# A feed-forward convolution placed three ticks later, with thirds of 3, 4 and 4 and one gate chunk ahead of the down-projection

## The chip, the cores and the metric

The kernel runs on one core of one Trainium2 chip. The core has a matmul engine (TensorE, PE in the profile), a vector engine (VectorE, DVE), a scalar engine (ScalarE, ACT), GpSimd (POOL) and SyncE (SP). Each takes its instructions in one fixed order and waits where an operand is not ready. ACT, SP and POOL also issue DMA transfers, which run on 16 DMA engines. The metric is the device time of one execution in microseconds; the median of three runs is compared.

## The reference

Two decoder layers over 256 rows of 2048 numbers. In each layer four attention groups are followed by a gated feed-forward block, and the change is in that block alone:

```python
def causal_depthwise_conv(u, w, bias):
    seq = u.shape[1]
    up = jnp.pad(u, ((0, 0), (CONV_WIDTH - 1, 0), (0, 0)))
    out = bias.astype(u.dtype) + up[:, 0:seq] * w[0]
    for j in range(1, CONV_WIDTH):
        out = out + up[:, j:j + seq] * w[j]
    return out

def ffn_sublayer(x, ffn_norm, w_up, conv_w, conv_b, w_down):
    h = rms_norm(x, ffn_norm)
    u = causal_depthwise_conv(h @ w_up, conv_w, conv_b)
    gate, val = jnp.split(u, 2, axis=-1)
    return x + (jax.nn.silu(gate) * val) @ w_down
```

`w_up` is 2048 x 11264: 5632 gate columns, then 5632 value columns. The convolution runs along the 256 rows, with three taps.

## The kernel before

Everything is float32. A product is made of three matmuls in a reduced format: weights and activations are split into a high and a low part, and high x high, low x high and high x low are added (L269 to L271). The activations' parts are made once. The weights' parts are made on the way: ACT casts a pair of weight tiles to the high part (L242, 1024 numbers a partition), DVE subtracts for the low part (L243). Four pairs of parts can be in flight (`wspl`, 4 buffers), and three raw weight loads of 1 MB, each of two pairs (`wraw`, 3 buffers; SP issues them).

A `Gemm` of the up-projection makes one chunk of 512 columns in 8 steps. A step takes one weight pair, issues 12 matmuls, and then calls `tick`. The 22 chunks of a layer are called g_0 to g_10 (gate) and v_0 to v_10 (value), and are taken alternately. A chunk comes out with rows on partitions, while convolution and down-projection want columns on partitions. So each chunk is turned: ACT evacuates it from PSUM with a row scale (L301, tile `v`), DVE transposes 32 x 32 blocks (L845, `T`), one DMA writes `T` to DRAM (L848, `td`) and four DMAs read it back turned (L853, `u`). `conv_T` then computes bias and last tap on ACT (L876), the other two taps on DVE (L878, L880), in two halves of two column blocks each. A gate chunk gets its SiLU (L885). A value chunk is multiplied with its gate chunk and split for the down-projection (L891 to L893, tiles `a0h_f`, `a0l_f` and so on).

What is not a Gemm step is written as tasks (generators). There are two queues: `movers` holds the turns, `queue` the convolutions and what follows them. A tick advances the first task of each queue to its next `yield`, with a bound that its instructions stand no earlier than the last matmul issued (`issue_after`). So a yield is one Gemm step. A scheduler then sets each engine's order from the program's order and those bounds, with its own cost estimates; ACT and DVE make weight parts ahead of TensorE as far as the four buffers go.

The columns are taken in thirds (`THIRDS`): chunks of a third, then its part of the down-projection (`paired`, L806), which adds to x. The down-projection of a third begins two column blocks (three in the last third) with the parts that are there, and takes the last part of each afterwards.

Of the kernel before, what the change touches and what calls it, by code (L numbers as in the profile page):

```python
# [29 lines left out]
NJ = DFF // 512  # L30
# [37 lines left out]
    _o += _w  # L68
CTW = _o

THIRDS = ((0, 4), (4, 8), (8, 11))


@with_exitstack
def tile_trunk(ctx: ExitStack, tc: tile.TileContext, x, xT, pvec, rows, ctab,
# [33 lines left out]
    queue, movers = deque(), deque()  # L109
# [7 lines left out]
    last_mm = [None]  # L117

    def tick(n=1):
        for _ in range(n):  # L120
            for q in (movers, queue):
                if q:
                    with tc.issue_after(last_mm[0].ins):
                        try:
                            next(q[0].gen)
                        except StopIteration:
                            q.popleft().done = True

    def finish(task):
        while task is not None and not task.done:  # L130
            tick()
# [38 lines left out]
    def act_slots(i, n):  # L170
        return slot(i, "h", [P, 4, SEQ], F32R, n), slot(i, "l", [P, 4, SEQ], F32R, n)
# [107 lines left out]
    def wchunk(w, k0=0):  # L279

        def src(raw, k, cnt, q=nc.sync):
            q.dma_start(raw[:, :cnt, :w.shape[2]], w[:, k0 + k:k0 + k + cnt, :])
        return src
# [14 lines left out]
    def evac(acc, n, N, rs, tag, bufs):  # L298
        d = tmp.tile([P, NT, 512], F32, tag=tag, name=f"{tag}_{n}", bufs=bufs)
        for t in range(NT):  # L300
            nc.scalar.activation(d[:, t, :N], acc[t][:, :N], AF.Identity, scale=rs[:, t:t + 1])  # L301
        return d
# [37 lines left out]
    def new_ssq(n):  # L340
        return sml.tile([P, NT, 4], F32, tag="ssq4", name=f"ssq4_{n}")
# [123 lines left out]
    def new_r(n):  # L465
        return sml.tile([P, NT], F32, tag="xs_r", name=f"r_{n}")

    def qk_tile(n):
        return tmp.tile([P, H, SEQ], F32, tag="qkT", name=f"qkT_{n}", bufs=3)
# [6 lines left out]
    for l in range(L):  # L476
# [99 lines left out]
        def gemm512(n, col, r, tag="qk", bufs=2, before=None):  # L576
            acc = Gemm(f"{n}{l}", 512, hT, wc[col], KT).run()
            finish(before)
            return evac(acc, f"{n}{l}", 512, r, tag, bufs)
# [14 lines left out]
        d = gemm512("aq", "aq", rs)  # L594
# [112 lines left out]
        d = gemm512("ak", "ak", rs)  # L707
# [79 lines left out]
        d = gemm512("cq_", "cq", rs, before=t_bq)  # L787
        qcT = qk_tile(f"qc{l}")
        t_cq2 = Task(c_task(d, qcT, l, f"cq_{l}", "cq"))
        d = gemm512("ck_", "ck", rs, before=t_bk)  # L790
# [49 lines left out]
        def turn(u, d, n):  # L840


            T = tmp.tile([P, KT, 32, NT], F32, tag="y", name=f"T_{n}", bufs=1)
            for t in range(NT):
                nc.vector.transpose(T[:, :, :, t], u[:, t, :].rearrange("p (b c) -> p b c", c=32))  # L845
            yield
            td = dram.tile([P, KT * 64], F32, tag="td", name=f"td_{n}")
            nc.scalar.dma_start(td, T.rearrange("p b c t -> p (b c t)"))  # L848
            yield
            yield  # L850
            src = td.rearrange("(a i) (c b x) -> b i c a x", i=32, b=4, x=64)
            for b in range(4):
                nc.scalar.dma_start(d[b * 32:(b + 1) * 32].rearrange("p c (a x) -> p c a x", x=64), src[b])  # L853
            yield
            yield
            yield

        def up(n, j):

            acc = Gemm(f"up_{n}", 512, hT, wchunk(w_up[l, j]), KT).run()  # L860
            u = evac(acc, n, 512, reo, "v", 1)
            d = tmp.tile([P, 4, SEQ], F32, tag="qk", name=f"u_{n}", bufs=2)
            gen = turn(u, d, n)
            next(gen)
            return d, Task(gen, movers)

        def conv_T(u, r, n, half, j):

            d, turned = u
            while not turned.done:  # L870
                yield
            for c in range(4):
                if c == 2:
                    yield
                ch = half * 44 + j * 4 + c
                nc.scalar.activation(r[:, c, :], d[:, c, :], AF.Identity, scale=pcol(l, "cw", 2 * 88 + ch),  # L876
                                     bias=pcol(l, "cb", ch))
                nc.vector.scalar_tensor_tensor(r[:, c, 1:], d[:, c, :SEQ - 1], pcol(l, "cw", 88 + ch), r[:, c, 1:],  # L878
                                               op0=ALU.mult, op1=ALU.add)
                nc.vector.scalar_tensor_tensor(r[:, c, 2:], d[:, c, :SEQ - 2], pcol(l, "cw", ch), r[:, c, 2:],  # L880
                                               op0=ALU.mult, op1=ALU.add)

        def gate_task(d, g, j):
            yield from conv_T(d, g, f"g{l}_{j}", 0, j)
            nc.scalar.activation(g, g, AF.Silu)  # L885

        def val_task(d, v, g, j, hi, lo):
            yield from conv_T(d, v, f"v{l}_{j}", 1, j)
            yield
            for c in (0, 2):  # L890
                nc.vector.tensor_tensor(v[:, c:c + 2, :], v[:, c:c + 2, :], g[:, c:c + 2, :], op=ALU.mult)  # L891
                nc.scalar.copy(hi[:, c:c + 2, :], v[:, c:c + 2, :])
                nc.vector.tensor_tensor(lo[:, c:c + 2, :], v[:, c:c + 2, :], hi[:, c:c + 2, :].bitcast(F32),  # L893
                                        op=ALU.subtract)

        last_layer = l == L - 1
        ssq_x, rs = new_ssq(f"n{l}"), new_r(f"n{l}")
        t_g = t_v = None
        for ti, (j0, j1) in enumerate(THIRDS):
            act, tasks = [], []  # L900
            for j in range(j0, j1):
                d = up(f"g{l}_{j}", j)
                finish(t_g)
                g = qk_tile(f"g{l}_{j}")
                t_g = Task(gate_task(d, g, j))
                finish(t_v)
                d = up(f"v{l}_{j}", NJ + j)
                v = qk_tile(f"v{l}_{j}")
                act.append(act_slots(j - j0, f"f{l}_{j}"))
                t_v = Task(val_task(d, v, g, j, *act[-1]))  # L910
                tasks.append(t_v)

            def post_down(c, acc):
                add_x(c, acc)
                if ti < 2:
                    return
                if last_layer:
                    for t in range(NT):
                        eng = nc.sync if t == 0 else nc.scalar
                        eng.dma_start(out[t * P:(t + 1) * P, c * 512:(c + 1) * 512],  # L920
                                      xs[:, t, c * 512:(c + 1) * 512])
                else:
                    h_task[c] = Task(x_ready(c, f"n{l}", "attn", l + 1, ssq_x, rs))
            nk = (j1 - j0) * 4
            paired(f"dn{l}_{ti}", slotted(act, tasks), w_down[l], j0 * 4, tuple(range(0, nk, 4)), nk, post_down,
                   3 if ti == 2 else 2)
# [72 lines left out]
```

## Time and profile before

| What | Value |
|---|---|
| median of 3 runs | 2359.29 us (2357.53 to 2368.61) |
| the profiled execution | 2353.14 us, with a span of 2351.4 us |
| mean granted clock of TensorE | 0.987 |
| busy: TensorE, DVE, ACT | 2262.7, 1450.2, 1171.0 us |
| HBM traffic over the span | 195 GB/s |
| ACT idle before L876, until u had landed | 117.4 us (gate) and 107.0 us (value), 22 times each |

A group's row names its line, engine, operation, output and inputs, shapes and count; behind the bar stand its busy time, the mean of one in ns, and the idle time of the engine just before these instructions with what ended it. In a row of stretches, the start and end of the stretch are followed by its length, the busy time and count of PE, PEld, DVE, ACT and POOL, the granted clock, the DMA engines' share and GB/s. ACTq and SPq are the issue of DMA transfers by ACT and SP. Busy time of matmuls overlaps, since they are pipelined: one lasts 0.39 us, and the next starts 0.227 us after it.

### The profile page before, as it was taken

What the parts mean: (1) busy time and instruction counts of PE and PEld (TensorE: products, weight loads), DVE (VectorE), ACT (ScalarE), POOL (GpSimd) and SP (SyncE); (2) the same over time, 40 slices, a digit from 0 to 9 for tenths busy, and PEclk for the clock granted to TensorE, in tenths of its full rate; (3) what the DMA queues carried; (4) which work ended last, traced back from release to release, by engine and by line L of the source; (5) the groups of instructions that cost most, each with busy time, mean ns of one, the idle gap of its engine ahead of it and who ended that gap; (6) DMA issues with size and microseconds to landing.
All of it is one profiled execution on the core that took longest, in us unless ns stands there. A gap on an engine that the chain in (4) does not pass through costs nothing.

```text
span 2351.4 us, 27050 instructions
## 1 busy us (share of the span) xinstructions
PE 2262.7 (96%) x10196; PEld 1853.5 (79%) x10196; DVE 1450.2 (62%) x2071; ACT 1171.0 (50%) x1651; POOL 3.9 (0%) x11
## 2 busy tenths in 40 slices
PE   9999999998999999988999999999999998999998
PEld 8888888777787777877888888887777876778777
DVE  6875865656555655465658757656565456564655
ACT  7555554545444544454556555545454345444543
POOL 0000000000000000000000000000000000000000
PEclk9999999999999999999999999999999999999999
DMA  8535545776657675667655445467766676756674
GB/s 315 197 126 171 173 162 160 241 226 185 209 199 229 197 221 191 200 198 208 200 168 191 139 166 166 158 178 229 218 203 209 201 211 190 229 195 210 207 223 144
DMA packets 163987, 460.83 MB, mean 196 GB/s; under 512 B 100496, under 2 KB 106000, under 8 KB 115728
## 3 DMA queue, kind: packets, MB, share of 16 engines
q1 hardware_dynamic: 63744, 411.63, 52.3%
q10 hardware_dynamic: 99984, 47.46, 9.2%
q8 instruction: 80, 1.31, 0.2%
q14 instruction: 51, 0.42, 0.1%
q0 software_dynamic: 128, 0.00, 0.0%
HBM read 433.89 MB, written 25.17 MB: 195 GB/s over the span
## 4 chain that ended last, share of the span: by engine, by line
PE 56%; DMA 23%; DVE 10%; ACT 4%; ACTq 4%; issue 2%; SPq 0%; DVEq 0%; POOLq 0%
DMA u_g<-td_g 8%; DMA u_v<-td_v 8%; PE acc_dn L271 5%; PE acc_dn L270 5%; PE acc_dn L269 5%; ACTq L853 3%; DMA td_v<-T_v 3%; DMA td_g<-T_g 2%; PE acc_out L269 2%; PE acc_out L270 2%; PE acc_out L271 2%; DVE qkT_v L878 2%; PE acc_up_g L271 2%; PE acc_up_g L269 2%; PE acc_up_g L270 2%
## 5 line engine op out<-in xcount | busy, mean ns | idle before, releaser
L271 PE MATMUL acc_up_v<-lo_up_v,hTs 128*128 128x512 f32 x704 | 279.2, 400 | 35.2 <-DVE lo_up_v L243 35.2
L243 DVE TENSOR_TENSOR lo_dn<-raw_dn,hi_dn 128x1024 fp32r<-128x1024 f32 x176 | 212.2, 1222 | 151.3 <-ACT hi_dn L242 151.1
L243 DVE TENSOR_TENSOR lo_up_g<-raw_up_g,hi_up_g 128x1024 fp32r<-128x1024 f32 x176 | 210.4, 1217 | 152.1 <-ACT hi_up_g L242 146.2
L243 DVE TENSOR_TENSOR lo_up_v<-raw_up_v,hi_up_v 128x1024 fp32r<-128x1024 f32 x176 | 208.9, 1220 | 144.3 <-ACT hi_up_v L242 144.3
L242 ACT CAST hi_dn<-raw_dn 128x1024 fp32r<-128x1024 f32 x176 | 182.3, 1053 | 211.7 <-PE acc_dn L270 180.5
L271 PE MATMUL acc_up_g<-lo_up_g,hTs 128*128 128x512 f32 x704 | 277.5, 394 | 10.3 <-DVE lo_up_g L243 10.2
L269 PE MATMUL acc_up_v<-hi_up_v,hTs 128*128 128x512 f32 x704 | 280.2, 398 | 6.0 <-ACT hi_up_v L242 6.0
L269 PE MATMUL acc_up_g<-hi_up_g,hTs 128*128 128x512 f32 x704 | 277.3, 394 | 7.1 <-ACT hi_up_g L242 7.1
L242 ACT CAST hi_up_v<-raw_up_v 128x1024 fp32r<-128x1024 f32 x176 | 180.8, 1052 | 201.4 <-PE acc_up_v L270 86.7
L270 PE MATMUL acc_up_v<-hi_up_v,hTs 128*128 128x512 f32 x704 | 280.0, 398 | 0.0
L270 PE MATMUL acc_up_g<-hi_up_g,hTs 128*128 128x512 f32 x704 | 276.0, 392 | 0.0
L242 ACT CAST hi_up_g<-raw_up_g 128x1024 fp32r<-128x1024 f32 x176 | 180.4, 1052 | 182.5 <-PE acc_up_g L270 58.5
L271 PEld LDWEIGHTS acc_up_v<-lo_up_v,hTs 128*128 128x128 f32 x704 | 135.0, 192 | 73.5 <-DVE lo_up_v L243 45.5
L271 PEld LDWEIGHTS acc_up_g<-lo_up_g,hTs 128*128 128x128 f32 x704 | 133.5, 190 | 42.3 <-DVE lo_up_g L243 14.5
L269 PEld LDWEIGHTS acc_up_v<-hi_up_v,hTs 128*128 128x128 f32 x704 | 135.5, 192 | 37.0 <-ACT hi_up_v L242 9.4
L269 PEld LDWEIGHTS acc_up_g<-hi_up_g,hTs 128*128 128x128 f32 x704 | 133.6, 190 | 37.3 <-ACT hi_up_g L242 10.0
L270 PEld LDWEIGHTS acc_up_v<-hi_up_v,hTs 128*128 128x128 f32 x704 | 135.9, 193 | 28.8
L270 PEld LDWEIGHTS acc_up_g<-hi_up_g,hTs 128*128 128x128 f32 x704 | 133.5, 190 | 27.5
L243 DVE TENSOR_TENSOR lo_out<-raw_out,hi_out 128x1024 fp32r<-128x1024 f32 x64 | 78.4, 1224 | 57.0 <-ACT hi_out L242 54.1
L876 ACT ACTIVATE qkT_g<-u_g,pv 128x256 f32<-128x256 f32 x88 | 46.0, 595 | 117.4 <-DMA u_g<-td_g 117.4
L878 DVE SCALAR_TENSOR_TENSOR qkT_g<-u_g,pv,qkT_g 128x255 f32<-128x255 f32 x88 | 40.6, 482 | 102.1 <-ACT qkT_g L876 101.9
L876 ACT ACTIVATE qkT_v<-u_v,pv 128x256 f32<-128x256 f32 x88 | 46.0, 596 | 107.0 <-DMA u_v<-td_v 107.0
(576 smaller groups left out, 4635.7 us busy)
## 6 DMA issues: line engine op xcount, KB each, us to landing
raw_up_g<-in_w_up_dram SPq DMA_DIRECT2D x88, 1024.0 KB, 5.6
raw_up_v<-in_w_up_dram SPq DMA_DIRECT2D x88, 1024.0 KB, 6.3
raw_dn<-in_w_down_dram SPq DMA_DIRECT2D x88, 1024.0 KB, 5.0
raw_out<-in_w_out_dram SPq DMA_DIRECT2D x32, 1024.0 KB, 4.8
td_g<-T_g ACTq DMA_DIRECT2D x22, 512.0 KB, 3.0
u_g<-td_g ACTq DMA_DIRECT2D x88, 128.0 KB, 7.5
td_v<-T_v ACTq DMA_DIRECT2D x22, 512.0 KB, 3.6
u_v<-td_v ACTq DMA_DIRECT2D x88, 128.0 KB, 8.9
```

Source lines behind the costliest of these rows:

```text
L242: nc.scalar.copy(h, r)
L243: nc.vector.tensor_tensor(w, r, h.bitcast(F32), op=ALU.subtract)
L269: nc.tensor.matmul(o, sh, wh, start=first, stop=False)
L270: nc.tensor.matmul(o, sl, wh, start=False, stop=False)
L271: last_mm[0] = nc.tensor.matmul(o, sh, wl_, start=False, stop=last)
L853: nc.scalar.dma_start(d[b * 32:(b + 1) * 32].rearrange("p c (a x) -> p c a x", x=64), src[b])
L876: nc.scalar.activation(r[:, c, :], d[:, c, :], AF.Identity, scale=pcol(l, "cw", 2 * 88 + ch), bias=pcol(l, "cb", ch))
L878: nc.vector.scalar_tensor_tensor(r[:, c, 1:], d[:, c, :SEQ - 1], pcol(l, "cw", 88 + ch), r[:, c, 1:], op0=ALU.mult, op1=ALU.add)
```

## The change

Four things are edited. A turn yields six times after its four reads rather than three, so a convolution becomes free to start three ticks later. A tick advances every turn that is under way rather than the first alone. The thirds are 3, 4 and 4 chunk pairs rather than 4, 4 and 3. And the first gate chunk of the next third is computed before the down-projection of this one; with it goes the rule that the next gate chunk's task starts only when the last one's is finished, while value chunks keep theirs.

```diff
-THIRDS = ((0, 4), (4, 8), (8, 11))
+THIRDS = ((0, 3), (3, 7), (7, 11))
...
     def tick(n=1):
         for _ in range(n):
-            for q in (movers, queue):
-                if q:
-                    with tc.issue_after(last_mm[0].ins):
-                        try:
-                            next(q[0].gen)
-                        except StopIteration:
-                            q.popleft().done = True
+            for task in [*movers, *list(queue)[:1]]:
+                with tc.issue_after(last_mm[0].ins):
+                    try:
+                        next(task.gen)
+                    except StopIteration:
+                        task.done = True
+                        (movers if task in movers else queue).remove(task)
...
-            yield
-            yield
-            yield
+            for _ in range(6):
+                yield
...
-        t_g = t_v = None
+        t_v, gates = None, {}
+
+        def start_gate(j):
+            g = qk_tile(f"g{l}_{j}")
+            Task(gate_task(up(f"g{l}_{j}", j), g, j))
+            gates[j] = g
+
         for ti, (j0, j1) in enumerate(THIRDS):
             act, tasks = [], []
             for j in range(j0, j1):
-                d = up(f"g{l}_{j}", j)
-                finish(t_g)
-                g = qk_tile(f"g{l}_{j}")
-                t_g = Task(gate_task(d, g, j))
+                if j not in gates:
+                    start_gate(j)
+                d = up(f"v{l}_{j}", NJ + j)
                 finish(t_v)
-                d = up(f"v{l}_{j}", NJ + j)
                 v = qk_tile(f"v{l}_{j}")
                 act.append(act_slots(j - j0, f"f{l}_{j}"))
-                t_v = Task(val_task(d, v, g, j, *act[-1]))
+                t_v = Task(val_task(d, v, gates[j], j, *act[-1]))
                 tasks.append(t_v)
+            if ti < 2:
+                start_gate(j1)
```

In the rows of the order, `g0_1` is the gate chunk 1 of layer 0; `hi_up_g0_2_4` is the high part of the weight pair at row block 4 for gate chunk 2; `qkT` is the convolution's output. The first place is ACT around the convolution of gate chunk 1, before:

```order
L848 DMA td_g0_1_4162<-T_g0_1_4138 128x1024
L242 CAST hi_up_v0_1_10_4236<-raw_up_v0_1_8_4218 128x1024
L853 DMA u_g0_1_4137<-td_g0_1_4162 32x16x64 x4
L242 CAST hi_up_v0_1_12_4260<-raw_up_v0_1_12_4258 128x1024
L242 CAST hi_up_v0_1_14_4283<-raw_up_v0_1_12_4258 128x1024
L876 ACTIVATE qkT_g0_1_4141<-u_g0_1_4137,pv_82 128x256 x4
L242 CAST hi_up_g0_2_0_4313<-raw_up_g0_2_0_4311 128x1024
L242 CAST hi_up_g0_2_2_4331<-raw_up_g0_2_0_4311 128x1024
L242 CAST hi_up_g0_2_4_4349<-raw_up_g0_2_4_4347 128x1024
L885 ACTIVATE qkT_g0_1_4141<-qkT_g0_1_4141 128x1024
L301 ACTIVATE v_v0_1_4299<-acc_up_v0_1_0_4142,reo_0_2810 128x512
```

And in the changed kernel:

```order
L853 DMA u_g0_1_4120<-td_g0_1_4144 32x16x64 x4
L242 CAST hi_up_v0_1_12_4254<-raw_up_v0_1_12_4252 128x1024
L242 CAST hi_up_v0_1_14_4270<-raw_up_v0_1_12_4252 128x1024
L242 CAST hi_up_g0_2_0_4301<-raw_up_g0_2_0_4299 128x1024
L875 ACTIVATE qkT_g0_1_3959<-u_g0_1_4120,pv_82 128x256 x2
L242 CAST hi_up_g0_2_2_4325<-raw_up_g0_2_0_4299 128x1024
L875 ACTIVATE qkT_g0_1_3959<-u_g0_1_4120,pv_82 128x256 x2
L242 CAST hi_up_g0_2_4_4350<-raw_up_g0_2_4_4348 128x1024
L301 ACTIVATE v_v0_1_4286<-acc_up_v0_1_0_4124,reo_0_2810 128x512
```

The first half of the convolution moved behind the first cast of the next chunk, the second half behind its second cast. The convolution still stands ahead of the evacuation of the next chunk (`v_v0_1`). The SiLU, no longer in these rows, stands behind both evacuations.

The second place is DVE at the same convolution, before:

```order
L878 SCALAR_TENSOR_TENSOR qkT_g0_1_4141<-u_g0_1_4137,pv_82,qkT_g0_1_4141 128x255 x2
L880 SCALAR_TENSOR_TENSOR qkT_g0_1_4141<-u_g0_1_4137,pv_82,qkT_g0_1_4141 128x254 x2
L878 SCALAR_TENSOR_TENSOR qkT_g0_1_4141<-u_g0_1_4137,pv_82,qkT_g0_1_4141 128x255 x2
L880 SCALAR_TENSOR_TENSOR qkT_g0_1_4141<-u_g0_1_4137,pv_82,qkT_g0_1_4141 128x254 x2
L243 TENSOR_TENSOR lo_up_g0_2_0_4314<-raw_up_g0_2_0_4311,hi_up_g0_2_0_4313 128x1024
L243 TENSOR_TENSOR lo_up_g0_2_2_4332<-raw_up_g0_2_0_4311,hi_up_g0_2_2_4331 128x1024
L845 STREAM_TRANSPOSE T_v0_1_4303<-v_v0_1_4299 128x512
L243 TENSOR_TENSOR lo_up_g0_2_4_4350<-raw_up_g0_2_4_4347,hi_up_g0_2_4_4349 128x1024
L845 STREAM_TRANSPOSE T_v0_1_4303<-v_v0_1_4299 128x512
```

And in the changed kernel:

```order
L243 TENSOR_TENSOR lo_up_g0_2_0_4302<-raw_up_g0_2_0_4299,hi_up_g0_2_0_4301 128x1024
L877 SCALAR_TENSOR_TENSOR qkT_g0_1_3959<-u_g0_1_4120,pv_82,qkT_g0_1_3959 128x255 x2
L879 SCALAR_TENSOR_TENSOR qkT_g0_1_3959<-u_g0_1_4120,pv_82,qkT_g0_1_3959 128x254 x2
L243 TENSOR_TENSOR lo_up_g0_2_2_4326<-raw_up_g0_2_0_4299,hi_up_g0_2_2_4325 128x1024
L877 SCALAR_TENSOR_TENSOR qkT_g0_1_3959<-u_g0_1_4120,pv_82,qkT_g0_1_3959 128x255 x2
L845 STREAM_TRANSPOSE T_v0_1_4290<-v_v0_1_4286 128x512
L879 SCALAR_TENSOR_TENSOR qkT_g0_1_3959<-u_g0_1_4120,pv_82,qkT_g0_1_3959 128x254 x2
L243 TENSOR_TENSOR lo_up_g0_2_4_4351<-raw_up_g0_2_4_4348,hi_up_g0_2_4_4350 128x1024
L845 STREAM_TRANSPOSE T_v0_1_4290<-v_v0_1_4286 128x512
```

From the first tap of the convolution to the second transpose of the next chunk there stood eight taps, three splits and two transposes; now there are eight taps, two splits and two transposes.

The third place is ACT at the start of the first down-projection in the changed kernel, where the gate chunk g0_3 of the next third has gone ahead and the value chunk v0_2 is the last of this third:

```order
L242 CAST hi_up_g0_3_14_4775<-raw_up_g0_3_12_4757 128x1024
L242 CAST hi_dn0_0_0_0_4804<-raw_dn0_0_0_0_4802 128x1024
L875 ACTIVATE qkT_v0_2_4630<-u_v0_2_4626,pv_82 128x256 x2
L242 CAST hi_dn0_0_0_2_4828<-raw_dn0_0_0_0_4802 128x1024
L875 ACTIVATE qkT_v0_2_4630<-u_v0_2_4626,pv_82 128x256 x2
L242 CAST hi_dn0_0_0_4_4852<-raw_dn0_0_0_4_4850 128x1024
L301 ACTIVATE v_g0_3_4791<-acc_up_g0_3_0_4634,reo_0_2810 128x512
```

Before, the last convolution of a third (v0_3) stood eight casts into the down-projection, and no chunk of the next third had begun.

## The prediction

> **What bounds the kernel now.** I read the page first, then the elapsed time of the feed-forward thirds, then the chain of waits in one stalled stretch.
>
> ```profile
> span 2351.4 us, 27050 instructions
> PE 2262.7 (96%) x10196; PEld 1853.5 (79%) x10196; DVE 1450.2 (62%) x2071; ACT 1171.0 (50%) x1651; POOL 3.9 (0%) x11
> ...
> L271 PE MATMUL acc_up_v<-lo_up_v,hTs 128*128 128x512 f32 x704 | 279.2, 400 | 35.2 <-DVE lo_up_v L243 35.2
> ...
> L876 ACT ACTIVATE qkT_g<-u_g,pv 128x256 f32<-128x256 f32 x88 | 46.0, 595 | 117.4 <-DMA u_g<-td_g 117.4
> ...
> L876 ACT ACTIVATE qkT_v<-u_v,pv 128x256 f32<-128x256 f32 x88 | 46.0, 596 | 107.0 <-DMA u_v<-td_v 107.0
> ```
>
> TensorE is 96% busy, so 88.7 us at most look free by the page. But busy time hides slow matmuls, and elapsed time shows more. In the next view each row is a stretch, its length, then busy time of each engine. The first six are the thirds of the feed-forward (up chunks and down-projection) of layer 0, then 1; the seventh is a layer's first up chunk, the eighth a chunk that nothing stalls.
>
> ```profile
> 391.66:676.06 284.40, 270.76 (x1162) 219.44 (x1161) 167.43 (x210) 135.42 (x168) 1.42 (x2) 0.98 0.68 207
> 676.06:959.91 283.85, 270.35 (x1154) 219.48 (x1152) 164.78 (x201) 130.62 (x157) 0.00 (x0) 0.98 0.66 208
> 959.91:1179.08 219.17, 205.56 (x889) 167.21 (x888) 130.28 (x165) 107.46 (x141) 0.00 (x0) 0.98 0.66 203
> 1564.52:1847.85 283.33, 268.96 (x1162) 218.32 (x1160) 167.38 (x210) 135.30 (x168) 1.28 (x2) 0.99 0.68 208
> 1847.85:2133.43 285.58, 268.72 (x1154) 218.16 (x1152) 164.96 (x201) 131.10 (x157) 0.00 (x0) 0.98 0.66 206
> 2133.43:2347.24 213.81, 202.92 (x865) 164.34 (x863) 121.67 (x150) 95.01 (x114) 0.00 (x0) 0.98 0.63 196
> ...
> 391.66:414.37 22.71, 22.71 (x105) 18.81 (x104) 12.20 (x19) 11.56 (x18) 1.42 (x2) 1.00 0.74 164
> ...
> 676.06:697.82 21.76, 21.76 (x98) 18.02 (x97) 11.09 (x11) 9.15 (x10) 0.00 (x0) 1.00 0.57 194
> ```
>
> An unstalled chunk of 96 matmuls takes 21.76 us, 2.72 us for each of its 8 steps. A third of four pairs is 8 chunks and a down-projection of 4 x 96 matmuls, 12 x 21.76 = 261.1 us; a third of three is 9 x 21.76 = 195.8. The six rows exceed that by 23.3, 22.7, 23.3, 22.2, 24.5 and 18.0, together 134 us. About 5 us of these are transposes for the norms: 8, 24 and 8 of them by the counts, at the 0.95 us that eight add in the seventh row. So stalls cost 129 us, and 2353.1 - 129 = 2224 us is the floor for a change that only moves feed-forward work. The matmuls themselves stay.
>
> Why do they stall? The chain of waits, in order of time (start, us, what), in the last third:
>
> ```profile
> 2221.89 0.61 ACT qkT_g L876
> 2222.53 0.48 DVE qkT_g L878
> ...
> 2225.88 1.14 DVE lo_up_g L243
> ...
> 2229.02 0.95 DVE lo_up_g L243
> 2230.12 0.71 DVE T_v L845
> 2230.86 3.35 DMA td_v<-T_v
> 2234.23 0.56 ACTq L853
> ...
> 2236.30 8.68 DMA u_v<-td_v
> 2245.01 0.61 ACT qkT_v L876
> ```
>
> This is a loop. The convolution of one chunk starts when its turned copy u has landed (2221.89). ACT and DVE work through it and through some weight splits before they reach the next chunk's evacuation and transposes (T_v, 2230.12); only then can that chunk start its trip through DRAM, which ends in its convolution (2245.01). One lap: 8.97 us from convolution to td, 14.15 us from td to the next convolution. First and last laps of two thirds, with the first trips (ACT in order of time):
>
> ```profile
> 700.76 0.33 ACTq L848 DMA_DIRECT2D td_g<-T_g  x1
> ...
> 714.59 2.09 ACT L876 ACTIVATE qkT_g<-u_g,pv 128x256 f32<-128x256 f32 x4 [2.39 <-DMA u_g<-td_g]
> ...
> 723.56 0.33 ACTq L848 DMA_DIRECT2D td_v<-T_v  x1
> ...
> 738.70 2.09 ACT L876 ACTIVATE qkT_v<-u_v,pv 128x256 f32<-128x256 f32 x4 [4.23 <-DMA u_v<-td_v]
> ...
> 2171.90 2.09 ACT L876 ACTIVATE qkT_g<-u_g,pv 128x256 f32<-128x256 f32 x4 [2.46 <-DMA u_g<-td_g]
> ...
> 2295.12 2.10 ACT L876 ACTIVATE qkT_v<-u_v,pv 128x256 f32<-128x256 f32 x4 [5.14 <-DMA u_v<-td_v]
> ```
>
> The last third has 5 laps in 2295.12 - 2171.90 = 123.22 us, 24.64 each. TensorE needs 21.76, so each lap drifts 2.9 us, and when the initial lead is gone TensorE pays it. Check: a third of four has 7 laps, 7 x 2.9 = 20 us, against 22.7 lost in the second. The loop, not any one wait, is the bound.
>
> **The change part by part.** Instruction counts on every engine are equal, DMAs too (one td and four u issues a chunk), so nothing is added or removed; what counts is order.
>
> *Later convolution.* In the order, the first half of a convolution now stands behind the first split of the next chunk on ACT and DVE, the second half behind the second split. Two things follow. First, conv to td has one weight split fewer in it. DVE's rows:
>
> ```profile
> 2222.53 0.98 DVE L878 SCALAR_TENSOR_TENSOR qkT_g<-u_g,pv,qkT_g 128x255 f32<-128x255 f32 x2 [6.63 <-ACT qkT_g L876]
> ...
> 2225.01 0.87 DVE L880 SCALAR_TENSOR_TENSOR qkT_g<-u_g,pv,qkT_g 128x254 f32<-128x254 f32 x2
> 2225.80 2.35 DVE L243 TENSOR_TENSOR lo_up_g<-raw_up_g,hi_up_g 128x1024 fp32r<-128x1024 f32 x2
> 2228.38 0.71 DVE L845 STREAM_TRANSPOSE T_v<-v_v 128x512 f32<-128x512 f32 x1 [0.23 <-ACT v_v L301]
> 2229.02 1.18 DVE L243 TENSOR_TENSOR lo_up_g<-raw_up_g,hi_up_g 128x1024 fp32r<-128x1024 f32 x1
> ```
>
> Now: 0.64 us until DVE starts, eight taps in 3.3 (2222.53 to 2225.80), three splits of about 1.1, two transposes of about 0.7, and two short gaps: 8.97. After: the same with two splits, 8.0 by my sum. A value chunk loses its product from that stretch instead; I take 8.0 for both.
>
> Second, TensorE tolerates a later landing. Before, the next chunk's first split waits: its lo is ready 5.1 us after the convolution starts (2225.80 plus half of 2.35, from 2221.89) and is needed about 0.45 us into the chunk, behind two matmuls. After, the first split is already done. The second is ready 0.64 + 4 x 0.41 + 1.15 = 3.5 us after the convolution, needed one step later, at 3.2; the third at 7.3, needed at 5.9; the fourth, behind a value's product, near 10.4, needed at 8.6. So the convolution must start 1.8 us before the chunk boundary, not 4.7. The first convolution of the second third starts at 714.59, its boundary is 697.82 + 21.76 = 719.58: 5.0 us ahead. The lead to use up becomes 5.0 - 1.8 = 3.2 us a third, from 0.3.
>
> What does not change is the structure: convolution still precedes the next evacuation on both engines. So the lap after is 8.0 plus the trip. The wait on u now has the second split, the second half and the evacuations behind it on ACT, DVE's taps follow; TensorE has one more step in hand.
>
> *The trip's length* is the unknown. Quiet end: 714.59 - 700.76 = 13.8 us, with TensorE unstalled. Crowded end: 24.64 - 8.97 = 15.7. The second trip of that third, right after the quiet one, is 738.70 - 723.56 = 15.1. The change smooths the splits (two halves, not three splits in a burst), so weight loads are released more evenly, but it also brings them faster. I take the middle, 14.7, as no row decides. The Trainium skill, DMA: Bandwidth & Descriptors, Queues, rings and completion order, says that each DMA engine takes turns between queues packet by packet; by it, the turn's small packets always lose time to weight loads, and the lap would sit at the crowded end (the 2284 of rival 1); the quiet 13.8 of this trace does not agree, the later 15.1 does.
>
> *Laps.* Convolutions per third were 8, 8, 6; now 7, 8, 7 with the gate chunk ahead. Laps: 19 a layer, both times. At 8.0 + 14.7 = 22.7 the drift is 0.94, a layer loses 19 x 0.94 - 3 x 3.2 = 8.3 us, both 17. At 13.8 the lap is 21.8 and nothing is lost; at 15.7 it is 23.7, 2 x (19 x 1.94 - 9.6) = 54 us.
>
> *Gate chunk ahead, thirds.* The last value convolution falls in steps 1 to 3 of the down-projection and is needed at step 9; before, steps 6 to 8 and step 13. Both leave at least five steps, 13 us or so, so I cost it at nothing; without that cover one step would show, 2.7 us a third. SP's queue gets the same loads in another order. *Overlapping turns* only lets one turn's last tick meet the next one's first: nothing.
>
> **Sum.** Stalls 129 less 17 gives 112 us: 2353.1 - 112 = 2241 for a profiled execution; the median of the runs is 6.2 us above that one, so 2247.
>
> **Rivals.** (1) *The loop stays as it is*: the trip keeps 15.7, saving 129 - 54 = 75, 2284. For it: the crowded trips, and weights will come faster. Against: the burst of splits is gone. (2) *The loop stops binding*: no stall is left, 2359.3 - 129 = 2230. For it: first trips in each third; against: the 15.1. (3) *Slower, by crowding*: with TensorE steadier, one more weight load falls inside each trip.
>
> ```profile
> q1 hardware_dynamic: 63744, 411.63, 52.3%
> ...
> raw_up_v<-in_w_up_dram SPq DMA_DIRECT2D x88, 1024.0 KB, 6.3
> ...
> u_v<-td_v ACTq DMA_DIRECT2D x88, 128.0 KB, 8.9
> ...
> DMA to landing us min/median/max: 3.4/8.6/14.5
> ```
>
> A load of 1.05 MB takes all 16 engines 1.05 x 0.523 x 2351 / 411.6 = 3.1 us. The trip becomes 18.8, the lap 26.8, the stalls 2 x (19 x 5.04 - 9.6) = 172 us: 2359.3 + 43 = 2402. It decides above a trip of 17.7, where 19 laps lose the present 129. For it: u's 128 KB take longer to land (8.9) than a load of eight times the size (6.3), and the last row shows landings of up to 14.5. Against: that is a maximum, the median is 8.6. By the rule of the Trainium skill named above this would be the common case. (4) *The change does nothing*: ACT reaches a convolution early anyway and the lead is spent at once; 2359.
>
> **How the numbers follow.** Forecast 0.42, rival 1 0.28, rival 2 0.18, rival 3 0.06, rival 4 0.06. The range holds the first three: 2229 to 2290, forecast, both bounds and a few us for the residue. Faster by over 0.5% (12 us, about what a measurement here can tell) is the first three, 0.88; within, 0.06; slower, 0.06.
>
> **What would show it.** Right: chunk lengths near 21.76 in the first four or five chunks of a third and 22 to 23 later; ACT's wait for u shorter than 5 us a time and still there; conv to td 8.0; the six thirds exceeding their matmuls by some 20 us in sum; granted clock 1.00 there where it was 0.98. Wrong: conv to td still near 9 (order), or trips above 16 us (crowding), or stalls in the down-projection at step 9 (thirds).

## The result, and the profile after

The changed kernel takes 2224.85 us (median of 4 runs, 2224.77 to 2226.07) against 2358.41 us before (4 runs, 2352.76 to 2368.61): 0.943 of the time, with a 95% interval of 0.9398 to 0.9463. The forecast was 2247 in a range from 2229 to 2290. The direction and the place of the gain were right, but the time came out below the range: no stall is left at all, which was rival 2.

From the page of the changed kernel: span, busy time of the engines, the chain that ended last by engine, and the groups that had waited.

```profile
span 2222.6 us, 27073 instructions
PE 2215.8 (100%) x10196; PEld 1839.2 (83%) x10196; DVE 1452.1 (65%) x2071; ACT 1192.0 (54%) x1651; POOL 3.9 (0%) x11
...
PE 99%; DVE 0%; DMA 0%; ACT 0%; issue 0%; SPq 0%; DVEq 0%; ACTq 0%
...
L271 PE MATMUL acc_up_v<-lo_up_v,hTs 128*128 128x512 f32 x704 | 273.9, 389 | 0.0
```

TensorE's busy time went from 96% to 100% of the span, and the chain that ended last is TensorE alone. The group L271 had 35.2 us of idle time ahead of it and a mean of 400 ns; now it has none and 389 ns. TensorE's idle time fell from 88.7 to 6.8 us, and its busy time itself by 46.9 us, since the matmuls got shorter: that part the busy share had hidden. Together these are the 128.8 us by which the span is shorter.

The six thirds of the two layers, in the form of the prediction's windows (length, then busy time and count of PE, PEld, DVE, ACT, POOL, granted clock, DMA share, GB/s):

```profile
391.58:610.13 218.55, 218.55 (x970) 181.03 (x968) 141.64 (x180) 117.44 (x144) 1.42 (x2) 1.00 0.74 226
610.13:871.25 261.12, 261.12 (x1154) 216.29 (x1153) 165.12 (x201) 135.18 (x157) 0.00 (x0) 1.00 0.71 226
871.25:1113.45 242.20, 242.20 (x1082) 200.64 (x1081) 156.59 (x195) 130.96 (x165) 0.00 (x0) 1.00 0.70 221
1498.88:1717.42 218.54, 218.54 (x969) 180.97 (x968) 141.54 (x180) 118.05 (x144) 1.28 (x2) 1.00 0.73 226
1717.42:1978.54 261.12, 261.12 (x1153) 216.22 (x1152) 165.47 (x201) 135.12 (x157) 0.00 (x0) 1.00 0.72 226
1978.54:2218.06 239.52, 239.52 (x1057) 198.01 (x1055) 148.00 (x180) 119.30 (x138) 0.00 (x0) 1.00 0.68 215
sum 1441.05, PE 1441.05 PEld 1193.16 DVE 918.37 ACT 756.06 POOL 2.70; mean PE 240.18 PEld 198.86 DVE 153.06 ACT 126.01 POOL 0.45
```

With the gate chunk ahead, the thirds hold 10, 12 and 11 pieces of 96 matmuls in each layer, 66 x 21.76 = 1436.2 us in all. The sum is 4.9 above that. The 40 transposes for the norms come to 4.8, by the 0.95 us that eight of them add to a layer's first chunk, so no stall is left in these rows. Before, the same six rows summed to 1570.1 us. The difference is 129.1 us, and the profiled executions differ by 2353.14 - 2224.77 = 128.4. So all of the gain lies in the feed-forward thirds, and it is the whole stall that the prediction had counted there.

What became of the waits: first ACT's wait ahead of the convolution, then who waited for u's reads and how long they took to land, then the transfers with their median time to landing.

```profile
L875 ACT ACTIVATE qkT_v<-u_v,pv 128x256 f32<-128x256 f32 x88 | 48.3, 596 | 31.7 <-DMA u_v<-td_v 31.7
L875 ACT ACTIVATE qkT_g<-u_g,pv 128x256 f32<-128x256 f32 x88 | 48.2, 596 | 4.5 <-DMA u_g<-td_g 4.5
```

```profile
  ACT qkT_v L875: 31.7, 22
  ACT qkT_g L875: 4.5, 4
...
DMA to landing us min/median/max: 3.5/6.0/10.0
```

```profile
q1 hardware_dynamic: 63744, 411.63, 55.0%
...
raw_up_v<-in_w_up_dram SPq DMA_DIRECT2D x88, 1024.0 KB, 5.2
...
td_g<-T_g ACTq DMA_DIRECT2D x22, 512.0 KB, 2.6
u_g<-td_g ACTq DMA_DIRECT2D x88, 128.0 KB, 6.0
...
u_v<-td_v ACTq DMA_DIRECT2D x88, 128.0 KB, 5.8
```

The gate convolution's wait for u fell from 117.4 to 4.5 us, the value convolution's from 107.0 to 31.7. What is left costs TensorE nothing. The reads of u themselves land sooner: median 6.0 us instead of 8.6, maximum 10.0 instead of 14.5, and this although the weight queue q1 takes a larger share of the DMA engines than before (55.0% against 52.3%). The bytes are the same and the span is shorter.

One lap in the last third, ACT in order of time:

```profile
2068.41 0.33 ACTq L848 DMA_DIRECT2D td_g<-T_g  x1
...
2071.06 2.63 ACTq L853 DMA_DIRECT2D u_g<-td_g  x4
...
2079.16 1.06 ACT L242 CAST hi_up_g<-raw_up_g 128x1024 fp32r<-128x1024 f32 x1 [1.62 <-PE acc_up_v L270]
2080.12 1.09 ACT L875 ACTIVATE qkT_g<-u_g,pv 128x256 f32<-128x256 f32 x2
2081.88 1.06 ACT L242 CAST hi_up_g<-raw_up_g 128x1024 fp32r<-128x1024 f32 x1 [0.67 <-PE acc_up_v L270]
2082.84 1.09 ACT L875 ACTIVATE qkT_g<-u_g,pv 128x256 f32<-128x256 f32 x2
...
2090.17 0.33 ACTq L848 DMA_DIRECT2D td_v<-T_v  x1
```

From td to td these are 21.76 us, exactly TensorE's own period. The convolution has no bracket, so u had landed when ACT reached it; the casts wait for TensorE (`<-PE`), not the reverse. Its td to convolution is 11.71 us. In the crowded lap of the prediction (td_v at 2230.86, convolution at 2245.01) it was 14.15.

### The profile page after: what moved, and what is told of

It reads as the page before. It is cut to its first block, busy times and chain, and to the rows that moved or that the text cites. A ratio compares the mean times of both kernels' runs of the same rounds, so it can differ in the third digit from the quotient of the medians.

```text
span 2222.6 us, 27073 instructions
## 1 busy us (share of the span) xinstructions
PE 2215.8 (100%) x10196; PEld 1839.2 (83%) x10196; DVE 1452.1 (65%) x2071; ACT 1192.0 (54%) x1651; POOL 3.9 (0%) x11
## 4 chain that ended last, share of the span: by engine, by line
PE 99%; DVE 0%; DMA 0%; ACT 0%; issue 0%; SPq 0%; DVEq 0%; ACTq 0%
PE acc_dn L270 7%; PE acc_dn L269 7%; PE acc_up_g L271 7%; PE acc_dn L271 7%; PE acc_up_g L269 7%; PE acc_up_v L269 7%; PE acc_up_g L270 7%; PE acc_up_v L270 7%; PE acc_up_v L271 7%; PE acc_out L271 3%; PE acc_out L269 3%; PE acc_out L270 3%; PE acc_aq L269 1%; PE acc_bk L271 1%; PE acc_av L269 1%; PE acc_bk L269 1%
## 5 line engine op out<-in xcount | busy, mean ns | idle before, releaser
L242 ACT CAST hi_up_g<-raw_up_g 128x1024 fp32r<-128x1024 f32 x176 | 185.2, 1055 | 201.4 <-PE acc_up_v L270 66.4
L243 DVE TENSOR_TENSOR lo_up_v<-raw_up_v,hi_up_v 128x1024 fp32r<-128x1024 f32 x176 | 213.6, 1223 | 117.0 <-ACT hi_up_v L242 117.0
L271 PE MATMUL acc_up_g<-lo_up_g,hTs 128*128 128x512 f32 x704 | 273.9, 389 | 0.0
L269 PE MATMUL acc_up_v<-hi_up_v,hTs 128*128 128x512 f32 x704 | 273.9, 389 | 0.0
L270 PE MATMUL acc_up_v<-hi_up_v,hTs 128*128 128x512 f32 x704 | 273.9, 389 | 0.0
L271 PE MATMUL acc_up_v<-lo_up_v,hTs 128*128 128x512 f32 x704 | 273.9, 389 | 0.0
L271 PEld LDWEIGHTS acc_up_g<-lo_up_g,hTs 128*128 128x128 f32 x704 | 132.2, 188 | 27.5
L271 PEld LDWEIGHTS acc_up_v<-lo_up_v,hTs 128*128 128x128 f32 x704 | 132.2, 188 | 27.5
L269 PEld LDWEIGHTS acc_up_v<-hi_up_v,hTs 128*128 128x128 f32 x704 | 132.2, 188 | 27.4
L270 PEld LDWEIGHTS acc_up_v<-hi_up_v,hTs 128*128 128x128 f32 x704 | 132.2, 188 | 27.4
L242 ACT CAST hi_out<-raw_out 128x1024 fp32r<-128x1024 f32 x64 | 67.3, 1051 | 63.0 <-PE acc_out L270 46.5
L269 PE MATMUL acc_dn<-hi_dn,a0h_f 128*128 128x512 f32 x192 | 74.9, 390 | 0.0
L269 PE MATMUL acc_dn<-hi_dn,a1h_f 128*128 128x512 f32 x192 | 74.8, 389 | 0.0
```

The source lines that it names most:

```text
L242: nc.scalar.copy(h, r)
L243: nc.vector.tensor_tensor(w, r, h.bitcast(F32), op=ALU.subtract)
L269: nc.tensor.matmul(o, sh, wh, start=first, stop=False)
L270: nc.tensor.matmul(o, sl, wh, start=False, stop=False)
L271: last_mm[0] = nc.tensor.matmul(o, sh, wl_, start=False, stop=last)
```

## The experiments

Two readings stood against each other. By the first, the lap is a plain sum: convolution to td, plus a trip of a fixed length, and the change won by shortening the first or by moving where TensorE needs the result. By the second, the trip is the larger lever and depends on the weight loads that run beside it, so that what counts is when those loads are issued. In the table, "trip" is the mean time from td's issue to the convolution that reads its data. "Gaps" are those from the issue of each weight load of the up-projections to the next load, counted from the trace: their standard deviation, and how many of 176 are under 3 us. "Conv to td" is the value of most laps. The ratio is to the kernel before, run on the same chip beside it.

```
kernel                          us       ratio [95%]              conv to td   trip    gaps sd (under 3 us)
before                          2358.41  1                        8.8 to 9.0   15.46   3.35 (36)
the change                      2224.85  0.943  [0.9398,0.9463]   7.86 *       12.56   1.35 (1)
three yields                    2348.66  0.9985 [0.9948,1.0021]   9.0          15.39   3.23 (35)
later convolution alone         2225.74  0.9452 [0.9416,0.9489]   7.85 *       13.04   1.43 (2)
five yields                     2319.51  0.9841 [0.9795,0.9886]   8.1 to 8.6   15.79   2.73 (26)
later, early finish             2305.57  0.9778 [0.9728,0.9828]   8.2 / 10.9+  14.42   3.06 (32)
unsplit convolution             2269.53  0.9646 [0.96,0.9693]     7.0 or 7.5   15.46   2.28 (25)
half up weights                 2267.98  0.9624 [0.9585,0.9662]   -            12.39   2.58 (27)
half up and down weights        2228.04  0.9477 [0.9435,0.952]    -            11.48   2.57 (26)
unsplit, half up weights        2227.53  0.9453 [0.9412,0.9494]   -            12.89   1.43 (14)
two more reads                  2248.17  0.9562 [0.9523,0.9602]   7.9          14.37   1.99 (11)
four more reads                 2291.44  0.9741 [0.9698,0.9783]   7.9 or 8.4   15.25   2.41 (8)
* where the engines set it; up to 10.05 where ACT and DVE wait for TensorE
```

**Which part of the change carries it?** First the change with its convolution put back to where it was. Thirds, the gate chunk ahead, the overlapping turns and the later end of a value chunk's task stay.

```diff
-            for _ in range(6):
+            for _ in range(3):
                 yield
```

> The changed kernel with the three yields of before in place of six: thirds of 3, 4, 4, the gate chunk ahead, overlapping turns and the later end of the value parts stay, the convolution goes back to its old place. Theory A (the place of the convolution makes the whole gain): the loop is back, 19 laps a layer of some 24.6 us, 2340 to 2360 us. Rival B (thirds and the gate chunk ahead carry a good part): 2260 to 2310 us.

Measured: 2348.66 us, 0.9985 of the kernel before, and the interval holds 1. Its page:

```profile
PE 2261.0 (97%) x10196; PEld 1851.0 (79%) x10196; DVE 1449.5 (62%) x2071; ACT 1169.2 (50%) x1651; POOL 3.9 (0%) x11
...
L875 ACT ACTIVATE qkT_g<-u_g,pv 128x256 f32<-128x256 f32 x88 | 45.9, 592 | 116.5 <-DMA u_g<-td_g 116.5
```

ACT's wait is that of the kernel before (117.4). So the parts that stay give nothing that can be measured by themselves.

Then the reverse: the kernel before with the later convolution alone. The thirds stay 4, 4, 3 and no chunk goes ahead. The value task is finished behind the next value chunk, as in the change, and the overlapping tick comes with the six yields.

```diff
-            yield
-            yield
-            yield
+            for _ in range(6):
+                yield
...
-                finish(t_v)
                 d = up(f"v{l}_{j}", NJ + j)
+                finish(t_v)
```

> The kernel before with six yields, overlapping turns and value parts that are finished after the next value chunk; thirds of 4, 4, 3 and no gate chunk ahead. Theory A: all of the gain, 2223 to 2230 us, every up chunk at 21.76 us. Rival B: stalls come back where the last convolutions of a third meet the down-projection, 2250 us or more.

Measured: 2225.74 us, within 1 us of the whole change. So the later place of the convolution carries the whole gain, together with the tick and the moved `finish` that come with it; the thirds and the gate chunk ahead are not needed. In one place of this kernel a trip took 18.62 us and the chunk 24.30; the next chunk took 22.09, and those behind it were back at 21.76 with nothing done for it. In this one case, then, a late trip did not start the stalls again.

The edit of `finish` matters too. With the six yields and the tick, but the value task finished ahead of the next value chunk as before:

```diff
                 finish(t_v)
                 d = up(f"v{l}_{j}", NJ + j)
```

> The later convolution alone (2225.7 us) but with each value part finished before the next value chunk, as in the kernel before: the last ticks of a value part then run without Gemm steps between, and in the order a gate convolution falls back ahead of the last split of its chunk. Theory A (the place behind the first split is needed for every convolution): 2340 to 2380 us. Rival H (the value part's end is a detail): 2225 to 2250 us.

Measured: 2305.57 us, between the two ranges expected, so neither held. ACT's order in the trace shows that most convolutions no longer stand in the changed place. Of the value chunks' convolutions, 16 of 22 are again in one piece ahead of the next chunk's first split, which is where they stood before the change. Of the gate chunks', 16 of 22 are in one piece ahead of the last split of the value chunk. Convolution to td is 8.2 us behind the value chunks' and 10.9 to 13 behind the gate chunks'.

```profile
L875 ACT ACTIVATE qkT_g<-u_g,pv 128x256 f32<-128x256 f32 x88 | 46.4, 592 | 122.7 <-DMA u_g<-td_g 122.7
...
u_g<-td_g ACTq DMA_DIRECT2D x88, 128.0 KB, 8.5
td_v<-T_v ACTq DMA_DIRECT2D x22, 512.0 KB, 6.4
u_v<-td_v ACTq DMA_DIRECT2D x88, 128.0 KB, 5.5
```

The kernel before, for comparison:

```profile
u_g<-td_g ACTq DMA_DIRECT2D x88, 128.0 KB, 7.5
```

Gate reads land later than before the change (8.5 against 7.5). Value reads are as quick as in the change (5.5), but the value chunks' td, which precedes them, takes 6.4 us instead of 2.8. The loop stays crowded, with the crowd at another place. So the six yields have their full effect only with the moved `finish`, which is worth some 80 us here. The list of edits ahead of the prediction does not name it, though the diff there shows it: value chunks keep their rule, but a value chunk's task now has to be finished behind the next value chunk's steps and no longer ahead of them. Without the later place it gives nothing, since the three-yield kernel has it too.

**Is it the place or the number of ticks?** Five yields put the first half of a convolution ahead of the next chunk's first split again, and the second half behind it.

```diff
-            for _ in range(6):
+            for _ in range(5):
                 yield
```

> The changed kernel with five yields: the first half of the convolution stands ahead of the next chunk's first split and the second half behind it, so from convolution to td there are three splits again (9.0 us, as before) and TensorE tolerates a landing some 3 us ahead of the chunk's boundary. Theory A1 (the trip is short, about 12.5 us, whenever the splits are not bunched): a lap of 9.0 + 12.5 = 21.5 is under 21.76, 2223 to 2235 us. Rival A2 (the one split less and the later place were needed, trips stay near 15): a lap of 24, 2290 to 2330 us.

Measured: 2319.51 us. Convolution to td is 8.1 to 8.6 us, close to the 8.0 forecast for the change and not the 9.0 expected here, yet three quarters of the gain are gone, as the second of the two theories (A2) had it. From its last third, ACT in order of time:

```profile
2107.43 0.33 ACTq L848 DMA_DIRECT2D td_g<-T_g  x1
...
2114.74 2.00 ACT L242 CAST hi_up_v<-raw_up_v 128x1024 fp32r<-128x1024 f32 x2 [4.16 <-issue]
2123.27 1.10 ACT L875 ACTIVATE qkT_g<-u_g,pv 128x256 f32<-128x256 f32 x2 [6.54 <-DMA u_g<-td_g]
...
2131.91 0.33 ACTq L848 DMA_DIRECT2D td_v<-T_v  x1
...
2148.64 1.09 ACT L875 ACTIVATE qkT_v<-u_v,pv 128x256 f32<-128x256 f32 x2 [7.11 <-DMA u_v<-td_v]
```

The lap is 2148.64 - 2123.27 = 25.37 us: 8.64 from convolution to td, then a trip of 16.73. Casts come in pairs without a gap (x2), ahead of long waits for u. A stretch between convolution and td that is shorter by half a microsecond does not free the loop, then, as long as the trip stays long.

**Do the halves matter?** The change with its convolution in one piece, behind the first split:

```diff
-                if c == 2:
-                    yield
```

> The changed kernel without the yield between the halves of a convolution: all of it stands behind the next chunk's first split. From convolution to td there are two splits, 7.9 us as in the changed kernel, and the second split's low part is ready 5.1 us after the convolution starts, which asks for a landing 1.9 us ahead of the chunk's boundary, against 1.8. Theory A (lap and lead decide): 2223 to 2232 us. Rival F (the halving is what spreads the splits and keeps weight loads apart): 2270 us or more.

Measured: 2269.53 us. Convolution to td is 7.0 or 7.5 us in all but a few laps (in the first lap below 2056.76 - 2048.80 = 7.96), mostly shorter than in the change, and still 45 us are lost. By the plain sum this kernel would have been no slower than the change, so that expectation missed; the 2270 of rival F is met within half a microsecond.

```profile
2048.80 2.08 ACT L873 ACTIVATE qkT_v<-u_v,pv 128x256 f32<-128x256 f32 x4 [0.16 <-DMA u_v<-td_v]
...
2056.76 0.33 ACTq L848 DMA_DIRECT2D td_g<-T_g  x1
...
2072.36 2.08 ACT L873 ACTIVATE qkT_g<-u_g,pv 128x256 f32<-128x256 f32 x4 [3.37 <-DMA u_g<-td_g]
```

The trip is 15.60 us here and 15.46 in the mean, as before the change.

**Is it the weight loads that make the trip long?** The kernel before, with each load of up-projection weights halved to 512 KB and each half used twice. Instruction counts and matmuls are those of before, and in the traces PE, ACT, DVE and SP each have their instructions in the same order; half of the up-projection's weights is left out of the computation.

```diff
-            src(loaded[n, k], k, min(4, nk))
+            src(loaded[n, k], k, 2 if n[:3] == "up_" else min(4, nk))
...
-        raw = loaded[n, k - k % 4][:, k % 4:k % 4 + 2]
+        o = 0 if n[:3] == "up_" else k % 4
+        raw = loaded[n, k - k % 4][:, o:o + 2]
```

> The kernel before, order unchanged, but each weight load of the up-projection brings 512 KB and its two row blocks are used twice, so half of the up-projection's weights are left out; casts, matmuls and turns are as many as before. Theory C (the trip through DRAM is long because bunched weight loads crowd it): trips shorten from 15.7 to 12 or 13 us, the lap is about 21.5 to 22, 2230 to 2270 us. Rival D (the trip is as long as it is for other reasons, and order alone matters): 2330 to 2360 us.

Measured: 2267.98 us. With the convolution left where it was, two thirds of the loss are gone. 31 of the 44 trips are 9.8 to 13.3 us, and behind the first of a layer nearly all up chunks take 21.76 or 22.01 us. Of the other 13 trips (14.1 to 16.4 us), 12 are the last two of a third, where the down-projection begins. What is left stands in the down-projections, whose loads were still full size:

```profile
L272 PE MATMUL acc_up_v<-lo_up_v,hTs 128*128 128x512 f32 x704 | 273.2, 392 | 0.0
L272 PE MATMUL acc_dn<-lo_dn,a0h_f 128*128 128x512 f32 x192 | 77.5, 403 | 7.3 <-DVE lo_dn L244 7.3
L272 PE MATMUL acc_dn<-lo_dn,a1h_f 128*128 128x512 f32 x192 | 76.9, 401 | 9.4 <-DVE lo_dn L244 9.4
```

So these were halved as well (the same edit with `n[:2] in ("up", "dn")`; half of the down-projection's weights is left out too):

> The kernel before with half of the up-projection's and of the down-projection's weights left out (each load brings 512 KB, its row blocks are used twice). With the up-projection's alone halved, 43 us above the changed kernel were left, all in the down-projections. Theory C (bunched weight loads make the trip long): these go too, 2225 to 2235 us, with the order of before. Rival D (the down-projection stalls by the order of its own casts): 2255 to 2270 us.

Measured: 2228.04 us, the time of the change, with the order of before.

```profile
PE 99%; DVE 0%; DMA 0%; ACT 0%; issue 0%; SPq 0%; DVEq 0%; ACTq 0%
...
u_g<-td_g ACTq DMA_DIRECT2D x88, 128.0 KB, 6.0
...
u_v<-td_v ACTq DMA_DIRECT2D x88, 128.0 KB, 3.6
```

The mean trip is 11.48 us. And the unsplit convolution, which had kept its long trips, with halved up weights (left out as in the first of these):

> The unsplit convolution behind the first split (2269.5 us, conv to td 7.2 us, trips of 15.5) with half of the up-projection's weights left out, as before. Theory C (its trips are long because weight loads crowd them): trips near 12.5, a lap near 20, every up chunk within 0.3 us of 21.76; with full loads left in the down-projections 2225 to 2245 us. Rival G (two whole convolution pieces in a row delay ACT and DVE, loads or not): 2255 to 2270 us.

Measured: 2227.53 us instead of 2269.53, every up chunk 21.76 us. In all three the bytes alone were changed (here too every engine keeps its order), and the trip fell from 15.5 us to between 11.5 and 12.9. The weight traffic beside it is what makes the trip long.

**How much room has the change?** Here the turn of the changed kernel reads td additionally into a second place that nothing uses, ahead of the reads that matter: all four pieces once more, or two of them.

```diff
-            for b in range(4):
-                nc.scalar.dma_start(d[...], src[b])
+            for o in (d2, d):
+                for b in range(4):
+                    nc.scalar.dma_start(o[...], src[b])
```

> The changed kernel, each turn reading its data back twice: four more reads of the same size into a scratch area in DRAM go out ahead of the four that count. That adds about 2.7 us of issue and some 2 us of transfer to the trip, 12.4 to about 17 us. Theory A (a lap of 7.9 us plus the trip that is over 21.76 us locks the kernel into the late regime): a lap near 25, 2300 to 2350 us. Rival E (the later place alone gives TensorE enough slack, whatever the trip): 2224 to 2240 us.

> As the run with four more reads, with two: a trip of about 14.8, a lap of 22.7, the lead of some 3.2 us a third is used up in three or four laps. Theory A: 2235 to 2300 us, between the changed kernel and the one with four more. Rival E: 2224 to 2230 us.

Measured: 2291.44 us with four more reads, just below the range of 2300 to 2350; 2248.17 with two, inside the range of 2235 to 2300. The mean trips are 15.25 and 14.37 us. So with a trip that is 1.8 us longer 23 us are lost again, and with one that is 2.7 us longer 67. These runs do not say that the length of the trip alone did it, since the additional reads are also issued by ACT. To issue the reads of one turn, from the first to the last, takes ACT 7.8 us in the mean with four more reads and 6.0 with two more, against 2.9 in the change, and with four more the issues are 9% of the chain that ended last:

```profile
PE 67%; DMA 12%; ACTq 9%; ACT 5%; DVE 5%; issue 2%; SPq 0%; DVEq 0%
```

Once it gets to a convolution, ACT waits 1.0 us for u there, about as in the change (0.8; before it was 5.1). What the two runs do show is that the changed kernel runs at TensorE's pace without much to spare on this path.

## Why the prediction was wrong

**What was right.** The bound was the loop from convolution to evacuation and transposes, td, the trip and the next convolution, and it was set against TensorE's 21.76 us. The 129 us of stalls were right to the microsecond: 2353.1 - 129 = 2224 was called the floor, and the profiled execution took 2224.8. Convolution to td was forecast at 8.0 us and is 7.86 where the engines set it. The granted clock is 1.00, as forecast. Thirds, gate chunk ahead and overlapping turns were costed at nothing; put in by themselves they give 0.9985, and the first two, left out of the change, are missed by less than 1 us. (Overlapping turns were not left out alone.) Rival 3, crowding to 2402, and rival 4, no effect, did not come.

**What failed is the term of the trip, 14.7 us.** It makes 17 of the 22 us by which the forecast was too long. The prediction took the middle between a quiet end of 13.8 and a crowded end of 15.7, "as no row decides". Measured is 12.56, below both ends. With it the loop's own lap is 7.86 + 12.56 = 20.4 us in the mean, shorter than TensorE's 21.76, so there is no lasting drift, and the 17 us of residue that were left in the sum are zero. Single laps are longer (a value chunk's trip of 14.85 makes 22.7), but the gate chunks' trips, 11.8 in the mean, make up for them. The chunks that were to take 22 to 23 us later in a third take 21.76. The lead and its deadlines (3.2 us a third instead of 0.3) needed no arithmetic, since nothing used the lead up.

**Why the bound itself was wrong.** Both ends came from the kernel before, and were treated as bounds on a constant. The quiet end was not quiet, either: 13.8 was read at the first trip of a third because TensorE had no stall there, but two weight loads were issued beside that td, and it took 6.3 us to land. From the kernel before, 700 to 707 us:

```profile
raw_up_g<-in_w_up_dram SPq DMA_DIRECT2D x2, 1024.0 KB, 6.5
td_g<-T_g ACTq DMA_DIRECT2D x1, 512.0 KB, 6.3
```

In the change the first trip of a third is no shorter (12.4 to 15.8 us); it is the others that are, 12.3 in the mean, and there td lands in 2.6 or 2.8 us (the medians above). So no trip that the prediction read was one without weight loads at its start.

The trip is an outcome of the same loop. On SP, where the weight loads are issued as soon as a raw buffer is free, one stretch of the kernel before:

```profile
720.87 0.33 SPq L282 DMA_DIRECT2D raw_up_g<-in_w_up_dram  x1
724.71 24.23 SPq L282 DMA_DIRECT2D raw_up_v<-in_w_up_dram  x4
750.85 8.11 SPq L282 DMA_DIRECT2D raw_up_g<-in_w_up_dram  x3
```

and one of the kernel after:

```profile
652.29 0.33 SPq L282 DMA_DIRECT2D raw_up_v<-in_w_up_dram  x1
658.93 13.68 SPq L282 DMA_DIRECT2D raw_up_g<-in_w_up_dram  x4
679.38 14.99 SPq L282 DMA_DIRECT2D raw_up_v<-in_w_up_dram  x4
```

Before, four loads stretch over 24 us and then three come within 8. After, each group of four takes 14 to 15 us. Over all up-projections 36 of 176 gaps were under 3 us and 36 over 8; now it is 1 and 10. Counted in the 12 us behind each td, 2574 KB of weights moved before and 2057 now, and 2610 and 2613 in the unsplit and the five-yield kernel, which kept the long trips. In the first 3 us behind a gate chunk's td, 18 of the change's 22 gate trips had no weight bytes beside them at all, and none of the 22 before had fewer than 128 KB. The mean trip is 2.9 us shorter: 0.9 of it is td's landing, 0.6 the four issues on ACT (3.5 to 2.9 us) and 1.5 the landing behind the last of them.

The reading that fits these counts is a loop that feeds itself: a late convolution holds ACT and DVE, then several splits come in a burst, the burst frees raw buffers together, their loads run together, and they run beside the next trip, which makes the next convolution late. The change breaks this by letting a split through ahead of each half of the convolution. The halved loads break it at the other place, with the order of before. The last link, loads to trip, is shown by the halved loads; the links before it are read from order and counts.

In the working, the sentence that came nearest was that the change "smooths the splits, so weight loads are released more evenly, but it also brings them faster". The two were weighed as if they might cancel. The weight loads' share of the DMA engines did rise, 52.3% to 55.0%, as the second half says; it is the first half that decides. Rival 1, the trip at 15.7, is what the unsplit kernel did: its lap, mean trip and convolution to td are near those used there, and it took 2269.53 where 2284 stood for the rival.

The rule of the Trainium skill that the prediction had weighed (DMA: Bandwidth & Descriptors, Queues, rings and completion order: DMA engines take turns between queues packet by packet) would, as the prediction read it, put the lap at the crowded end always. The halved loads agree that u's packets lose time to the weight loads. The changed kernel does not agree with "always": over the run it moves more weight bytes per microsecond, but fewer in the 12 us behind a td, and its reads of u land in 6.0 us instead of 8.6.

**The offset to the median.** 6.2 us were added because the median of the runs before stood that far above the profiled execution. After, the median is 0.1 us above it, and four runs lie within 1.3 us, where those before spread over 16. The spread goes with the stalls: the four kernels of 2225 to 2228 us spread over 1.0 to 4.9 us, the others over 7.5 to 31. These 6.2 us account for the distance between rival 2's 2230 and the measured 2225. They took the result out of the range: with the trip right and the offset kept, the forecast would have been rival 2's number, inside it.

**What stays open.** That the bunching of loads, rather than their bytes, is what the change removes follows from the counts and from the unsplit kernel, which moves the same bytes and keeps the long trips. It was not tested by spacing the loads by hand in the order of before. Six yields without the overlapping tick were not run. Where the early finish puts the convolutions was read from one trace, and how much of the loss with more reads is the longer trip and how much ACT's issues stays open.

## What to carry to other kernels

When a loop through in-order engines and DRAM is longer than the bottleneck engine's period, do not bound its DMA latency by what the slow kernel shows, since that latency can be produced by the loop's own lateness, and look at what else the DMA engines carried in the trip that you take for the quiet one; ask whether there is a second, even state, and what its lap would be. A cheap test is to halve the bytes of the competing loads without touching the order: if the stall goes, the traffic beside the transfer is the lever, and smoothing it in time may do as much as removing it. Let the next unit's prefetch work through ahead of, and between the pieces of, an operation that waits for a long transfer.

## What the runs showed that was not expected

- The same 128 KB reads of u land in 5.6 to 6.0 us (median) when full weight loads are issued evenly (the change, the later convolution alone), and in 7.5 to 9.1 in the four kernels (before, three yields, five yields, unsplit) that bunch them and read td no more than once; with the loads of up- and down-projection halved the value chunks' reads take 3.6 us, the gate chunks' 6.0. The 1 MB weight loads themselves change less (from 5.6 and 6.3 to 5.2 us).
- A shorter stretch on ACT and DVE can come with a longer time: the unsplit convolution has 7.0 or 7.5 us from convolution to td in most laps against 7.86 for the halves, and is 45 us slower.
- The granted clock was 0.98 in all but one of the stalled thirds, and 0.99 in that one. It is 1.00 in all six without stalls, and the mean matmul of L271 fell from 400 to 389 ns with it. The trace before has the clock at 0.50 for 63 us in all, in stretches of at most 6.8 us (one from 484.40 to 487.81 us), though no idle time of TensorE was longer than 3.3 us; the trace after has 5 us, at the very end. So the gain of 129 us is larger than the 88.7 us in which TensorE was idle before.
